# The end of a routed-expert diffusion step: the last expert's 128 rows gathered and normed apart from the other latents

## Chip, cores and metric

The kernel runs on one core of a Trainium2 chip. The metric is the device time of one execution in microseconds; three runs of the kernel before gave 2111.43 us as median (2108.97 to 2113.84).

## The reference, cut to what matters

One layer is computed for 128 prompt tokens and 1024 latent tokens of width 1024. The part that the change touches is the end of the mixture of experts and the final norm:

```python
gate, idx = lax.top_k(jnp.swapaxes(aff, 1, 2), cap)       # each of 16 experts picks its own 128 latents (16 prompt tokens)
xs  = h[idx]
hid = silu(xs @ w1[e]) * (xs @ w3[e])                     # 1024 -> 2048
out = (hid @ w2[e]) * gate[..., None]                     # 2048 -> 1024
y   = zeros.at[idx].add(out)                              # a token can be picked by several experts, or by none
x   = x + gate2 * y
y_prompt, y_sample = rmsnorm(x_prompt, final_g), rmsnorm(x_sample, final_g)
```

A latent that the last expert didn't pick has its final value once the fifteenth expert's rows are added. At most 128 of the 1024 latents change after that.

## The kernel before

`hybrid_step_kernel` first runs the token mixer and the routing (to about 800 us), and then a loop over the 16 experts (`for e in range(E)`), each with two products. The first makes the hidden units in four blocks `fb`, for `w1` and `w3`. The second makes the 1024 outputs in two halves `dh`, each in four steps `kq` over the 2048 hidden units; `n = 4 * dh + kq` counts them from 0 to 7. Weights come as 384 chunks of 1 MB over the SP queue into five `raw` buffers. ScalarE casts each to a high part (`split_hi`, L1291), VectorE takes the rest as a bf16 low part (`split_lo`, L1297), and the buffer that this frees gets the next load. `ahead(n)` does the splits that come before chunk `n`. TensorE multiplies high parts (`highs`, L1482) and low parts (`lows`, L1492) into PSUM; `sums` copies the low half out on ScalarE (`bs`, L1502) and adds it on VectorE (`ot`, L1503). Every engine executes its instructions in the order in which the program writes them (`tc.manual_schedule()`), so this order is set by hand.

`finish(e, ot)` turns an expert's outputs into rows: TensorE transposes, VectorE scales by the gate, and GpSimd's indirect DMA adds the 128 rows to `x3_d`, the latents in HBM (L1516). For the last expert (`e == E - 1`) the end is made differently:

- `last_hot` (GpSimd) builds one-hot matrices that place the 128 rows among the eight latent tiles of 128 rows.
- After step `n = 3`, `last_half` adds columns 0 to 511 to `x3_d` by an indirect DMA (L1568), and the eight loads of L1575 fetch the latents from there; they wait for that addition to land.
- `last_rows` and `last_add` place columns 512 to 767 (during the second half of the product) and 768 to 1023 (after it) by matmuls with the one-hot matrices (L1554) and add them to the tiles in SBUF (L1556).
- Then the eight latent tiles get their sums of squares (L1544, L1782, L1789), the norm's small steps (`go3`, L149 to L157), the multiplication by the norm and `final_g` (`last_out`: L1776 on VectorE, for tiles 4 and 8 L1773 on ScalarE and L1774 on GpSimd) and their stores (L1777).
- The prompt's second group of eight experts is added by `finish_prompt` (L1598 to L1607); the prompt's norm and store (L1815, L1816) are the last work.

Of the kernel before, what the change touches and what calls it, by code (L numbers as in the profile page):

```python
# [8 lines left out]
F32 = mybir.dt.float32  # L9
# [10 lines left out]
P = 128  # L20
# [29 lines left out]
def hybrid_step_kernel(ctx: ExitStack, tc: tile.TileContext, x_prompt, x_sample, state_lru, c, c_ctx,  # L50
# [114 lines left out]
    ss3 = const.tile([P, NT], F32, name="ss3")  # L165
    rs1, go1 = rms(ss1, "a", NT)
    rs2, go2 = rms(ss2, "b", NT)
    rs3, go3 = rms(ss3, "c", NT)
# [903 lines left out]
    tile1 = route.tile([P, 8], F32, name="tile1")  # L1072
    lgi2 = route.tile([P, 1], I32, name="lgi2")

    def constants():
# [8 lines left out]
        G.iota(tile1, pattern=[[P, 8]], base=-1, channel_multiplier=0, allow_small_or_imprecise_dtypes=True)  # L1084
# [76 lines left out]
    def list_make(pool, e, hot):  # L1161

        t = tp_tile()
        for i in range(8):
            PE.matmul(t[:, :5], hot[:, i, :], parts[:, i, e, :], start=i == 0, stop=i == 7)
        c = pool.tile([P, 8], F32, name="lc", bufs=1)
        V.tensor_copy(c[:, :5], t[:, :5])
        V.scalar_tensor_tensor(lgi[:, e:e + 1], c[:, 4:5], float(P), c[:, 3:4], op0=OP.mult, op1=OP.add)
        if e == E - 1:
            V.scalar_tensor_tensor(c[:, 5:6], c[:, 4:5], float(P), c[:, 3:4], op0=OP.mult, op1=OP.add)  # L1170
            V.tensor_scalar(lgi2, c[:, 5:6], 2.0, None, op0=OP.mult)
            V.tensor_scalar(tile1, tile1, c[:, 5:6], -1.0, op0=OP.subtract, op1=OP.mult)
        V.tensor_tensor(c[:, 6:7], c[:, 1:2], c[:, 2:3], op=OP.add)
        V.tensor_tensor(lgv[:, e:e + 1], c[:, 0:1], c[:, 6:7], op=OP.add)
# [345 lines left out]
    sq4 = ep.tile([P, 4, 3], F32, name="sq4")  # L1520
    last = {}

    def last_hot():
        last["oh"] = ew.tile([P, D], F32R, name="xg", tag="xg", bufs=1).rearrange("p (i t) -> p i t", i=8)
        for i in range(8):
            G.tensor_scalar(last["oh"][:, i, :], iof, tile1[:, i:i + 1], None, op0=OP.is_equal)
        jv = ep.tile([P, 2, 512], F32, name="jv", tag="x2")
        last["junk"], last["vals"] = jv[:, 0], jv[:, 1]

    def last_rows(ot, d0, d1):  # L1530

        n = (d1 - d0) * P
        cs = slice(d0 * P, d1 * P)
# [3 lines left out]
        v = last["vals"][:, :n]  # L1537
        V.scalar_tensor_tensor(v, t[:, :n], lgv[:, E - 1:], g2r[:, cs], op0=OP.mult, op1=OP.mult)
        last["hl"] = hl_ = ew.tile([P, 2, 512], F32R, name="rows", bufs=2)[:, :, :n]
        A.copy(hl_[:, 0], v)  # L1540
        V.tensor_tensor(hl_[:, 1], v, hl_[:, 0].bitcast(F32), op=OP.subtract)

    def last_square(i, d0, d1, c):
        A.activation(last["junk"][:, :(d1 - d0) * P], x3s[i // 2][:, i % 2, d0 * P:d1 * P], AF.Square,  # L1544
                     accum_out=sq4[:, i, c:c + 1])

    def last_add(t, i0, d0, d1, c):

        n = (d1 - d0) * P
        cs = slice(d0 * P, d1 * P)  # L1550
        m = 512 // n
        for i in range(m):
            for a in range(2):
                PE.matmul(t[:, i * n:(i + 1) * n], last["oh"][:, i0 + i, :], last["hl"][:, a], start=a == 0, stop=a == 1)  # L1554
        x = x3s[i0 // 2][:, i0 % 2:i0 % 2 + m, cs]
        V.tensor_tensor(x, x, t.rearrange("p (i d) -> p i d", i=m), op=OP.add)  # L1556
        if c == 1 and i0 < 4:
            for i in range(m):
                last_square(i0 + i, d0, d1, c)

    def last_half(ot):

        rows = ew.tile([P, D], F32, name="rows", bufs=2)[:, :512]
        t = tp_tile()
        for k in range(4):
            PE.transpose(t[:, k * P:(k + 1) * P], ot[:, k, :CAP], ident)
        V.scalar_tensor_tensor(rows, t, lgv[:, E - 1:], g2r[:, :512], op0=OP.mult, op1=OP.mult)
        G.indirect_dma_start(out=x3_d.rearrange("r (h d) -> (r h) d", h=2),  # L1568
                             out_offset=bass.IndirectOffsetOnAxis(ap=lgi2, axis=0),
                             in_=rows, in_offset=None, compute_op=OP.add)  # L1570
        for h in (1, 0):
            for p in range(4):
                if h:
                    x3s[p] = ew.tile([P, 8, 256], F32, name="raw", bufs=RB).rearrange("p a b -> p (a b)")                         .rearrange("p (i d) -> p i d", i=2)
                SY.dma_start(x3s[p][:, :, h * 512:(h + 1) * 512],  # L1575
                             x3_d[p * 2 * P:(p + 1) * 2 * P, h * 512:(h + 1) * 512].rearrange("(i p) d -> p i d", p=P))

    def last_sums(ot):
        for _ in range(4):
            yield  # L1580
        last_rows(ot, 4, 6)
        yield
        for i in (0, 4):
            last_add(tp_tile(), i, 4, 6, 1)
            last_add(tp_tile(), i + 2, 4, 6, 1)
            yield

    def finish_prompt(g):

        oh = ep.tile([P, P], F32R, name="oh")  # L1590
# [3 lines left out]
        for h in range(2):  # L1594
            pr.append(ew.tile([P, 2, 512], F32R, name="rows", bufs=2))
# [3 lines left out]
            A.activation(pr[h][:, 0], t, AF.Copy, scale=pgv[:, g:g + 1])  # L1599
            V.scalar_tensor_tensor(pr[h][:, 1], t, pgv[:, g:g + 1], pr[h][:, 0].bitcast(F32), op0=OP.mult, op1=OP.subtract)  # L1600
        yield
        for h in range(2):
            hs = slice(h * 512, (h + 1) * 512)
            t = tp_tile()
            for a in range(2):
                PE.matmul(t, oh, pr[h][:, a], start=a == 0, stop=a == 1)
            V.tensor_tensor(x2p[:, hs], x2p[:, hs], t, op=OP.add)  # L1607

# [23 lines left out]
    for e in range(E):  # L1632
# [73 lines left out]
        for dh in range(2):  # L1706
            for kq in range(4):
                n = 4 * dh + kq
                step = None if quarter is None else lambda r: next(quarter, None)
                if (e, dh) == (E - 1, 1):  # L1710
# [135 lines left out]
```

## Time and profile before

| | us |
|---|---|
| median of three runs | 2111.43 |
| the profiled execution, as timed | 2112.77 |
| its span in the trace | 2111.0 |
| PE busy in the span | 2043.4 |
| DVE busy in the span | 1710.9 |
| ACT busy in the span | 1366.0 |
| last matmul of the last expert's products ends | 2079.21 |

A line such as L1776 is a line of the kernel before; PE is TensorE, DVE VectorE, ACT ScalarE, POOL GpSimd, and SP the queue of the sync engine. Times in the trace count from the start of the span. PEclk is the share of full speed that TensorE was granted.

### The profile page before, as it was taken

How to read it: one execution, taken by the hardware profiler on the slowest of the kernel's cores; microseconds unless marked ns; L12 is line 12 of the kernel's file. 1: busy time of each engine (PE TensorE's matmuls, PEld its weight loads, DVE VectorE, ACT ScalarE, POOL GpSimd, SP SyncE). 2: the span in 40 equal slices, each digit the busy share in tenths (PEclk: the TensorE clock that was granted, in tenths of full speed). 3: DMA queues.
4: the chain of work that ended last, by engine and by line, in shares of the span. 5: the costliest groups of instructions: out<-in, count | busy, mean ns of one | idle time of the engine just before them, and what ended most of it. 6: DMA issues, size and time to landing. Idle time of an engine off the chain costs nothing.

```text
span 2111.0 us, 40842 instructions
## 1 busy us (share of the span) xinstructions
PE 2043.4 (97%) x17397; PEld 1968.8 (93%) x17397; DVE 1710.9 (81%) x1913; ACT 1366.0 (65%) x1442; POOL 203.6 (10%) x337
## 2 busy tenths in 40 slices
PE   7999999999999997999999999999999999999995
PEld 4899998999999876899999999999999999999994
DVE  7788988732236377999999999998999899999896
ACT  7477675322112236777877877877877887787783
POOL 0000001010102121010010010011011011001031
PEclk9999999999999998999999999999999999999997
DMA  8143434164655348999999999999999999999985
GB/s 271 57 120 117 125 116 121 52 203 144 189 168 178 118 145 306 317 323 323 345 337 325 344 329 330 348 349 326 335 345 325 345 348 329 343 342 332 344 310 184
DMA packets 304821, 543.93 MB, mean 258 GB/s; under 512 B 16299, under 2 KB 85627, under 8 KB 304638
## 3 DMA queue, kind: packets, MB, share of 16 engines
q1 hardware_dynamic: 285306, 478.56, 65.1%
q0 software_dynamic: 15728, 52.77, 8.6%
q10 hardware_dynamic: 3604, 9.98, 1.3%
q8 instruction: 136, 2.23, 0.4%
q14 instruction: 47, 0.39, 0.1%
HBM read 500.60 MB, written 40.67 MB: 256 GB/s over the span
## 4 chain that ended last, share of the span: by engine, by line
PE 88%; DVE 7%; DMA 2%; ACT 1%; issue 1%; SPq 0%; DVEq 0%; ACTq 0%; POOLq 0%
PE ac L1482 37%; PE ac L1492 17%; PE a L196 6%; PE a L197 6%; PE a L195 6%; PE a L778 5%; DVE lo L1297 2%; PE a L1002 2%; PE a L1004 2%; PE a L1003 2%; DMA xg<-hn_d,lgi 1%; PE tp L667 1%; PE tp L1420 1%; PE tp L1040 1%; PE tp L1513 1%
## 5 line engine op out<-in xcount | busy, mean ns | idle before, releaser
L1297 DVE TENSOR_TENSOR lo<-raw,hi 128x2048 bf16<-128x2048 f32 x384 | 872.0, 2284 | 0.0
L1291 ACT CAST hi<-raw 128x2048 fp32r<-128x2048 f32 x384 | 729.4, 1912 | 9.1 <-DMA raw<-in_exp_w_dram 7.1
L1482 PE MATMUL ac<-x,hi 128*128 128x288 f32 x4096 | 585.5, 298 | 0.0
L1482 PEld LDWEIGHTS ac<-x,hi 128*128 128x128 f32 x4096 | 549.0, 188 | 1.0 <-issue 0.9
L1492 PEld LDWEIGHTS <-lo 128*128 128x128 bf16 x6144 | 382.6, 98 | 16.2
L1482 PE MATMUL ac<-hh,hi 128*128 128x288 f32 x2048 | 297.7, 298 | 0.0
L1502 ACT COPY bs<-ac 128x288 f32<-128x288 f32 x320 | 127.6, 399 | 246.4 <-PE ac L1482 131.6
L1492 PE MATMUL ac<-xb,lo 128*128 128x144 bf16 x4096 | 282.5, 226 | 0.0
L1482 PEld LDWEIGHTS ac<-hh,hi 128*128 128x128 f32 x2048 | 275.5, 188 | 0.0
L197 PE MATMUL a<-hn_hi,lo 128*128 128x384 f32 x624 | 210.5, 337 | 1.9 <-DVE lo L186 1.9
L195 PE MATMUL a<-hn_hi,hi 128*128 128x384 f32 x624 | 210.4, 337 | 0.0
L196 PE MATMUL a<-hn_lo,hi 128*128 128x384 f32 x624 | 210.2, 337 | 0.0
L1492 PE MATMUL ac<-hb,lo 128*128 128x144 bf16 x2048 | 146.8, 226 | 0.0
L186 DVE TENSOR_TENSOR lo<-raw,hi 128x1024 fp32r<-128x1024 f32 (+1 forms) x77 | 88.3, 1164 | 64.4 <-ACT hi L185 64.4
L1503 DVE TENSOR_TENSOR h<-ac,bs 128x288 f32<-128x288 f32 x256 | 115.3, 450 | 20.1 <-ACT bs L1502 19.8
L197 PEld LDWEIGHTS a<-hn_hi,lo 128*128 128x128 f32 x624 | 117.7, 189 | 2.2 <-DVE lo L186 2.2
L195 PEld LDWEIGHTS a<-hn_hi,hi 128*128 128x128 f32 x624 | 118.0, 189 | 0.4
L196 PEld LDWEIGHTS a<-hn_lo,hi 128*128 128x128 f32 x624 | 118.0, 189 | 0.0
L185 ACT CAST hi<-raw 128x1024 fp32r<-128x1024 f32 (+1 forms) x77 | 75.9, 1002 | 46.8 <-PE a L196 36.6
L1759 POOL TENSOR_TENSOR yps<-ot,modc 128x128 f32<-128x128 f32 x16 | 36.0, 2248 | 720.0 <-DVE ot L1503 720.0
L1503 DVE TENSOR_TENSOR ot<-ac,bs 128x288 f32<-128x288 f32 x64 | 29.2, 457 | 56.5 <-ACT bs L1502 56.5
L701 ACT ACTIVATE sg<-a 128x1152 f32<-128x1152 f32 x16 | 18.2, 1135 | 78.9 <-PE a L197 78.8
(439 smaller groups left out, 2648.2 us busy)
## 6 DMA issues: line engine op xcount, KB each, us to landing
raw<-in_exp_w_dram SPq DMA_DIRECT2D x380, 1024.0 KB, 7.4
raw<-in_w_in_dram SPq DMA_DIRECT2D x28, 512.0 KB, 4.7
raw<-in_w_mod_dram SPq DMA_DIRECT2D x28, 512.0 KB, 5.8
araw<-in_w_mod_dram SPq DMA_DIRECT2D x18, 256.0 KB, 7.2
g_d<-sg ACTq DMA_DIRECT2D x8, 576.0 KB, 3.3
yh_d<-yh POOLq DMA_DIRECT2D x8, 576.0 KB, 3.1
yl_d<-yl POOLq DMA_DIRECT2D x8, 576.0 KB, 4.6
m_d<-sg POOLq DMA_DIRECT2D x8, 576.0 KB, 4.2
```

Source lines behind the costliest of these rows:

```text
L185: A.copy(h, raw)
L186: V.tensor_tensor(l, raw, h.bitcast(F32), op=OP.subtract)
L195: PE.matmul(out, whi, xhi, start=first, stop=False)
L196: PE.matmul(out, whi, xlo, start=False, stop=False)
L197: PE.matmul(out, wlo, xhi, start=False, stop=last)
L778: PE.matmul(a3[:, ch, :CH], w[:, k, :], y[:, k, cs], start=n == 0 and k == 0 and w is hi, stop=n == 1 and k == KD - 1 and w is ws[-1])
L1291: A.copy(hl[n][0], raw[n])
L1297: V.tensor_tensor(lo, r, hi.bitcast(F32), op=OP.subtract)
L1482: PE.matmul(a[:, r, :2 * S], w[0][:, k, c0 + r * P:c0 + (r + 1) * P], x2(kk), start=kk == first, stop=kk == last)
L1492: PE.matmul(a[:, r, S:2 * S], w[1][:, k, c0 + r * P:c0 + (r + 1) * P], xb(kk), start=False, stop=kk == last)
L1502: A.copy(b, a[:, :, S:2 * S])
L1503: V.tensor_tensor(dst, a[:, :, :S], b, op=OP.add)
```

## The change

The eight latent tiles, with the rows of the first fifteen experts, are loaded whole while the last expert's second product runs (`last_load`; the first load goes into the buffer of `x2`, the others into `raw` buffers). They are normed, multiplied by `final_g` in place and stored to `y_sample` (`last_squares`, `go3`, `last_out`), spread over the steps `n` by `last_step`. The last expert's 128 rows are gathered once from `x3_d` (`xe`); `last_cols` adds the expert's outputs to them in three column groups and takes their squares, and after the product they get a norm of their own and are scattered by an indirect DMA over the rows of `y_sample` that were already stored. The one-hot matrices, their matmuls and the two index tables that they needed are gone. `finish_prompt` multiplies with plain fp32 operands (two matmuls) in place of a high and a low part (four). At step `n = 3`, `last_cols`, `prompt_sums` and the first part of `finish_prompt` now stand ahead of the last `ahead`, and with it ahead of the last chunk's low part.

```diff
-    def last_half(ot):
...
-        G.indirect_dma_start(out=x3_d.rearrange("r (h d) -> (r h) d", h=2),
...
+    def last_loads():
+        last["fg"] = ep.tile([P, D], F32, name="fg", tag="xp")
+        A.dma_start(last["fg"], bass.AP(tensor=final_g.tensor, offset=final_g.offset, ap=[[0, P], [1, D]]))
+        last["junk"] = ew.tile([P, D], F32, name="rows", bufs=2)
+        last["vals"] = ep.tile([P, 512], F32, name="vals", tag="h0")
+        last_load(0)
+        last["xe"] = ep.tile([P, D], F32, name="xe", tag="xf")
+        G.indirect_dma_start(out=last["xe"], out_offset=None, in_=x3_d[:, :],
+                             in_offset=bass.IndirectOffsetOnAxis(ap=lgi[:, E - 1:E], axis=0))
+        last_load(1)
+        last_load(2)
+
+    def last_load(p):
+        if p:
+            x = ew.tile([P, 8, 256], F32, name="raw", bufs=RB).rearrange("p a b -> p (a b)").rearrange("p (i d) -> p i d", i=2)
+        else:
+            x = ep.tile([P, 2, D], F32, name="x30", tag="x2")
+        x3s[p] = x
+        SY.dma_start(x, x3_d[p * 2 * P:(p + 1) * 2 * P, :].rearrange("(i p) d -> p i d", p=P))
+
+    def last_squares(p):
+        for i in range(2):
+            A.activation(last["junk"], x3s[p][:, i], AF.Square, accum_out=ss3[:, 2 * p + i:2 * p + i + 1])
+
+    def last_out(p):
+        for i in range(2):
+            n, x = 2 * p + i, x3s[p][:, i]
+            V.scalar_tensor_tensor(x, x, rs3[:, n:n + 1], last["fg"], op0=OP.mult, op1=OP.mult)
+            SY.dma_start(y_sample[0, n * P:(n + 1) * P, :], x)
+
+    def last_cols(ot, d0, d1, c, early=None):
+        n, cs, xe = (d1 - d0) * P, slice(d0 * P, d1 * P), last["xe"]
+        t = tp_tile()
+        for k in range(d0, d1):
+            PE.transpose(t[:, (k - d0) * P:(k - d0 + 1) * P], ot[:, k, :CAP], ident)
+        if early is not None:
+            early()
+        V.scalar_tensor_tensor(last["vals"][:, :n], t[:, :n], lgv[:, E - 1:], g2r[:, cs], op0=OP.mult, op1=OP.mult)
+        V.tensor_tensor(xe[:, cs], xe[:, cs], last["vals"][:, :n], op=OP.add)
+        A.activation(last["junk"][:, :n], xe[:, cs], AF.Square, accum_out=sqe[:, c:c + 1])
+
+    def last_step(n):
+        if n == 0:
+            last_loads()
+        elif n == 1:
+            last_load(3)
+        elif n == 2:
+            last_squares(0)
+        elif n == 3:
+            last_squares(1)
+            go3(slice(0, 4))
+        elif n == 4:
+            last_out(0)
+            last_squares(2)
+        elif n == 5:
+            last_out(1)
+            last_squares(3)
+        elif n == 6:
+            last_cols(ot, 4, 6, 1)
+            go3(slice(4, 8))
+            last_out(2)
+            last_out(3)
...
-                ahead(base + kq + 1 + AH)
                 if (e, n) == (E - 1, 3):
-                    last_half(ot)
+                    last_cols(ot, 0, 4, 0)
+                    prompt_sums(0, G)
                     fp = finish_prompt(1)
                     next(fp)
-                    quarter = last_sums(ot)
...
+                ahead(base + kq + 1 + AH)
+                if e == E - 1:
+                    last_step(n)
...
+    fg, xe = last["fg"], last["xe"]
+    first = slice(0, 512)
     next(fp)
+    prompt_sums(1, V)
+    last_cols(ot, 6, 8, 2, lambda: (next(fp), V.tensor_tensor(xe[:, first], xe[:, first], fg[:, first], op=OP.mult)))
+    V.tensor_reduce(ss3[:, 9:10], sqe[:, 0:3], axis=AX.X, op=OP.add)
+    go3(slice(9, 10), (0,))
+    next(fp)
+    next(fp)
+    go3(slice(9, 10), (1,))
+    A.activation(xe[:, first], xe[:, first], AF.Copy, scale=rs3[:, 9:10])
+    V.scalar_tensor_tensor(xe[:, 512:], xe[:, 512:], rs3[:, 9:10], fg[:, 512:], op0=OP.mult, op1=OP.mult)
+    G.indirect_dma_start(out=y_sample[0], out_offset=bass.IndirectOffsetOnAxis(ap=lgi[:, E - 1:E], axis=0),
+                         in_=xe, in_offset=None)
+    next(fp)
+    next(fp)
+    V.tensor_tensor(x2p[:, first], x2p[:, first], fg[:, first], op=OP.mult)
+    V.tensor_tensor(ss3[:, 8:9], sqe[:, 3:4], sqe[:, 4:5], op=OP.add)
+    go3(slice(8, 9))
+    A.activation(x2p[:, first], x2p[:, first], AF.Copy, scale=rs3[:, 8:9])
+    V.scalar_tensor_tensor(x2p[:, 512:], x2p[:, 512:], rs3[:, 8:9], fg[:, 512:], op0=OP.mult, op1=OP.mult)
+    SY.dma_start(y_prompt[0], x2p)
```

How the order of the instructions moves is shown at three places. The line numbers of the changed kernel differ by a few: L1291 became L1284, L1297 L1290, L1502 L1495, L1503 L1496.

The first place is ScalarE at the start of the last expert's second product: the casts of the last three chunks (`hi`) and the PSUM copies (`bs`) of its first half. Before:

```order
L1703 ACTIVATE ready<-ready 1x1
L1291 CAST hi<-raw 128x2048 x3
L1502 COPY bs<-ac 128x288 x2
L1747 DMA raw<-in_final_g_dram 128x1024
L1502 COPY bs<-ac 128x288
L1540 CAST rows<-jv 128x256
```

Now:

```order
L1706 ACTIVATE ready<-ready 1x1
L1284 CAST hi<-raw 128x2048
L1519 DMA fg<-in_final_g_dram 128x1024
L1284 CAST hi<-raw 128x2048 x2
L1539 ACTIVATE rows,ss_110<-x_24389 128x1024 x2
L1495 COPY bs<-ac 128x288 x2
L1557 ACTIVATE rows,sqe<-xe 128x512
L1539 ACTIVATE rows,ss_110<-raw 128x1024 x2
L150 ACTIVATE rr_c<-rv_c 128x4
L1539 ACTIVATE rows,ss_110<-raw 128x1024 x2
L1495 COPY bs<-ac 128x288
```

Two squares of whole latent tiles stand ahead of the two copies of the first half, and five more squares ahead of the third copy.

The second place is VectorE where the first half's outputs (`ot`) are done and one chunk's low part (`lo`) is left. Before:

```order
L1297 TENSOR_TENSOR lo<-raw,hi 128x2048 x3
L1503 TENSOR_TENSOR ot<-ac,bs 128x288 x2
L1297 TENSOR_TENSOR lo<-raw,hi 128x2048
L1567 SCALAR_TENSOR_TENSOR rows<-tp,lgv,g2r 128x512
L1591 TENSOR_SCALAR oh<-iof,pgf 128x128
```

Now:

```order
L1290 TENSOR_TENSOR lo<-raw,hi 128x2048 x3
L1496 TENSOR_TENSOR ot<-ac,bs 128x288 x2
L1555 SCALAR_TENSOR_TENSOR vals<-tp,lgv,g2r 128x512
L1556 TENSOR_TENSOR xe<-xe,vals 128x512
L1590 TENSOR_SCALAR oh<-iof,pgf 128x128
L1290 TENSOR_TENSOR lo<-raw,hi 128x2048
```

The last low part moved behind the three operations on the expert's rows.

The third place is VectorE during the second half of the product, between the third and the last output sums; only the new order is shown, since nothing of it stood there before:

```order
L1496 TENSOR_TENSOR ot<-ac,bs 128x288
L1544 SCALAR_TENSOR_TENSOR raw<-raw,rr_c,fg 128x1024 x2
L1555 SCALAR_TENSOR_TENSOR vals<-tp,lgv,g2r 128x256
L1556 TENSOR_TENSOR xe<-xe,vals 128x256
L149 TENSOR_SCALAR rv_c<-ss_110 128x4
L153 RECIPROCAL rq_c<-rr_c 128x4
L154 TENSOR_TENSOR rq_c<-rq_c,rv_c 128x4
L155 TENSOR_TENSOR rq_c<-rq_c,rr_c 128x4
L156 TENSOR_SCALAR rq_c<-rq_c 128x4
L157 RECIPROCAL rr_c<-rq_c 128x4
L1544 SCALAR_TENSOR_TENSOR raw<-raw,rr_c,fg 128x1024 x4
L1496 TENSOR_TENSOR ot<-ac,bs 128x288
```

All eight multiplications of the latent tiles (two stand just ahead of the piece) come before the last `ot`, with which the work on the last quarter of the product begins.

## Rows read from the trace of the kernel before

**Rows 1.** Windows: us, busy of PE, PEld, DVE, ACT, POOL, granted clock, DMA share, GB/s

```profile
2050.00:2060.00 10.00, 10.00 (x108) 9.79 (x107) 10.00 (x6) 9.33 (x8) 0.00 (x0) 1.00 0.39 141
```

**Rows 2.** The chain that ended last, in order of time: start us, us, what

```profile
2072.46 7.96 DMA raw<-x_d
```

**Rows 3.** Timeline of PE, second half of the last product: start us, us, operation

```profile
2062.87 2.38 PE L1482 MATMUL ac<-hh,hi 128*128 128x288 f32 x16
2065.09 2.17 PE L1492 MATMUL ac<-hb,lo 128*128 128x144 bf16 x32
...
2077.99 1.22 PE L1482 MATMUL ac<-hh,hi 128*128 128x288 f32 x8
```

**Rows 4.** Timeline of ACT, end of the last product's first half

```profile
2053.84 5.51 ACT L1291 CAST hi<-raw 128x2048 fp32r<-128x2048 f32 x3
...
2061.73 0.40 ACT L1502 COPY bs<-ac 128x288 f32<-128x288 f32 x1 [1.21 <-PE ac L1482]
```

**Rows 5.** Timeline of DVE at the same place

```profile
2062.53 2.28 DVE L1297 TENSOR_TENSOR lo<-raw,hi 128x2048 bf16<-128x2048 f32 x1
2064.73 0.75 DVE L1567 SCALAR_TENSOR_TENSOR rows<-tp,lgv,g2r 128x512 f32<-128x512 f32 x1
...
2065.40 0.28 DVE L1591 TENSOR_SCALAR oh<-iof,pgf 128x128 fp32r<-128x128 f32 x1
```

**Rows 6.** Timeline of the latent tiles' multiplications and squares after the product

```profile
2089.25 1.28 DVE L1776 SCALAR_TENSOR_TENSOR hi<-raw,rr_c 128x1024 f32<-128x1024 f32 x1
2090.45 0.68 DVE L1556 TENSOR_TENSOR raw<-raw,ac 128x512 f32<-128x512 f32 x1
2090.47 1.04 ACT L1782 ACTIVATE hi<-raw 128x1024 f32<-128x1024 f32 x1
...
2091.64 1.06 ACT L1782 ACTIVATE hi<-raw 128x1024 f32<-128x1024 f32 x1
```

**Rows 7.** Timeline of the small steps, the last quarter's and the prompt's

```profile
2081.12 0.45 DVE L1503 TENSOR_TENSOR ot<-ac,bs 128x288 f32<-128x288 f32 x1
...
2082.10 0.48 DVE L1538 SCALAR_TENSOR_TENSOR jv<-tp,lgv,g2r 128x256 f32<-128x256 f32 x1 [0.53 <-PE tp L1536]
...
2083.68 0.63 ACT L1544 ACTIVATE jv<-raw 128x512 f32<-128x512 f32 x1
...
2096.52 0.15 DVE L149 TENSOR_SCALAR rv_c<-ss 128x4 f32<-128x4 f32 x1
...
2097.77 0.18 DVE L157 RECIPROCAL rr_c<-rq_c 128x4 f32<-128x4 f32 x1
...
2102.55 1.27 DVE L1607 TENSOR_TENSOR x2p<-x2p,tp 128x512 f32<-128x512 f32 x2
...
2106.54 1.41 DVE L1815 SCALAR_TENSOR_TENSOR hi<-x2p,rr_c,raw 128x512 f32<-128x512 f32 x2
2107.32 0.99 SPq L1816 DMA_DIRECT2D out_dram<-hi  x2
```

**Rows 8.** DMA issues after 1990 us: out<-in, queue, count, KB each, median us to landing

```profile
raw<-in_exp_w_dram SPq DMA_DIRECT2D x19, 1024.0 KB, 6.4
raw<-x_d SPq DMA_DIRECT2D x8, 512.0 KB, 7.5
out_dram<-hi SPq DMA_DIRECT2D x8, 512.0 KB, 3.2
...
out_dram<-hi SPq DMA_DIRECT2D x2, 256.0 KB, 2.0
```

**Rows 9.** Line 1516, all fifteen experts' indirect additions: us to landing

```profile
DMA to landing us min/median/max: 6.1/7.6/9.6
```

**Rows 10.** Timeline of SP: the last weight loads

```profile
2000.95 48.75 SPq L1285 DMA_DIRECT2D raw<-in_exp_w_dram  x16
```

**Rows 11.** Timeline of PE: plain fp32 at 20 us, high and low parts at 1492 us

```profile
20.54 3.60 PE L386 MATMUL tp<-araw,sil 128*4 128x512 f32 x8
...
1491.78 1.09 PE L1606 MATMUL tp<-rows,oh 128*128 128x512 f32 x4
```

More of the change, by code (lines that the diff above doesn't have):

```diff
@@ L164, in hybrid_step_kernel @@
     ss2 = const.tile([P, NT], F32, name="ss2")
-    ss3 = const.tile([P, NT], F32, name="ss3")
+    ss3 = const.tile([P, NT + 1], F32, name="ss3")
     rs1, go1 = rms(ss1, "a", NT)
     rs2, go2 = rms(ss2, "b", NT)
-    rs3, go3 = rms(ss3, "c", NT)
+    rs3, go3 = rms(ss3, "c", NT + 1)
     pa = ExitStack()
@@ L1517, in finish @@
                              in_=rows, in_offset=None, compute_op=OP.add)
-    sq4 = ep.tile([P, 4, 3], F32, name="sq4")
+    sqe = ep.tile([P, 16], F32, name="sqe")
     last = {}
[L1523 to L1533, printed above, removed]
+    def last_loads():
[26 more added lines that the diff above has]
+        n, cs, xe = (d1 - d0) * P, slice(d0 * P, d1 * P), last["xe"]
         t = tp_tile()
@@ L1536, in last_rows @@
             PE.transpose(t[:, (k - d0) * P:(k - d0 + 1) * P], ot[:, k, :CAP], ident)
[L1537 to L1559, printed above, removed]
@@ L1561, in last_half @@
-    def last_half(ot):
[L1563 to L1567, printed above, removed]
-        G.indirect_dma_start(out=x3_d.rearrange("r (h d) -> (r h) d", h=2),
[L1569 to L1576, printed above, removed]
@@ L1604, in finish_prompt @@
             t = tp_tile()
-            for a in range(2):
-                PE.matmul(t, oh, pr[h][:, a], start=a == 0, stop=a == 1)
+            PE.matmul(t, oh, pr[h], start=True, stop=True)
+            if g:
+                yield
             V.tensor_tensor(x2p[:, hs], x2p[:, hs], t, op=OP.add)
+            if g:
+                A.activation(last["junk"][:, :512], x2p[:, hs], AF.Square, accum_out=sqe[:, 3 + h:4 + h])
+                yield
     find = search(1, 5)
@@ L1779, in hybrid_step_kernel @@
-    junk = ew.tile([P, 8, 256], F32R, name="hi", bufs=HB).rearrange("p a b -> p (a b)")[:, :D].bitcast(F32)
-    def last_squares(x, i):
-        A.activation(junk, x, AF.Square, accum_out=ss3[:, i:i + 1])
-    for i in range(4):
-        last_square(i, 0, 4, 0)
-    for i in range(2):
-        last_square(i, 6, 8, 2)
-        x = x3s[1][:, i, 768:]
-        V.scalar_tensor_tensor(last["vals"][:, :256], x, 1.0, x, op0=OP.mult, op1=OP.mult, accum_out=sq4[:, 2 + i, 2:3])
-    V.tensor_reduce(ss3[:, 1:5], sq4, axis=AX.X, op=OP.add)
```

88 lines of the change are left out of this document (17 added, 71 removed).

## Prediction

> **What bounds the kernel now.** I read the page first: PE is busy for 2043 of 2111 us, so up to the end of the last product only what PE does or waits for counts. Then I read the end alone, by the chain that ended last, the timeline of each engine and the landing times. The last matmul of the products starts its group at 2077.99 us and ends at 2079.21 [rows 3]; the span ends at 2111.0. For these 31.8 us PE is no longer the bound: the chain goes through the loads of the latents (7.96 us of waiting [rows 2]), then through VectorE, which works off the last additions, nine multiplications, three norms and the prompt's rows, each in turn. So the question is what the change leaves behind the last product, and whether what it puts ahead of that delays the product itself. Room there is: between 2050 and 2060 us the DMA engines are 39% busy, and the last weights are through [rows 1, 10].
>
> **The product, step by step.** The loads of the latents go out behind the last weight load, at about 2049.7 us [rows 10]. A load lands 6.4 us (weights) to 7.5 us (latents) after its issue [rows 8], so the first is there at 2056 to 2057.5; the others wait for `raw` buffers, at most until the casts end. Cost: nothing, hidden behind the casts of the last three chunks, which end at 2053.84 + 5.51 = 2059.35 [rows 4]. Without that cover ScalarE would stand still (a rival, below).
>
> ScalarE then squares two tiles ahead of the PSUM copies. Squares follow each other at 1.17 us [rows 6]: 2059.35 + 2.34 = 2061.7, two copies of 0.40 end at 2062.5 in place of 2062.13 [rows 4]. PE, which waits for them, resumes 0.4 us later: 2063.3 in place of 2062.87 [rows 3].
>
> The last chunk's low part moves behind three VectorE operations: 0.75, then an addition that I price at 0.64 (half of the pair of 1.27 [rows 7]), 0.28, and then its own 2.28 [rows 5]. From 2063.3 that ends at 2067.2, in place of 2064.8. PE wants it after 16 high matmuls (2.22 us between two starts [rows 3]), 16 low ones (half of 2.17) and a few more: 2066.6. New stall: 0.6 us.
>
> In exchange the one-hot matmuls and PE's waits for loaded tiles leave the product. What is left of the second half is 4 x 2.22 + 2 x 2.17 = 13.2 us [rows 3], some 0.3 us of transposes and the stall: it ends at 2077.4, 1.8 us earlier than before.
>
> **VectorE beside it.** This is the term that decides. Low part done at 2067.2. ScalarE has by then squared the first group of the expert's rows (0.63 [rows 7]) from 2064.7 and two more tiles, until 2067.7. The norm's six small steps with ScalarE's root take from 2096.52 to 2097.95 in the rows, 1.43 us [rows 7]: 2069.1. Then the tiles' multiplications at 1.20 us each (2089.25 to 2090.45, with no GpSimd beside them [rows 6]): two end at 2071.5, the third `ot` (0.45 [rows 7]) at 2072.0, two more at 2074.4, the expert's columns 512 to 767 with two operations of 0.48 [rows 7] at 2075.4, square and norm again (0.6 + 1.43) at 2077.4, four more multiplications at 2082.2. Only then comes the last `ot`, done at 2082.65, though PE has had it ready since 2077.4. Before it ended at 2081.57. So the name of the change holds by half: the last two pairs of tiles are finished behind the product, and the last quarter leaves VectorE 1.1 us later than now.
>
> **The tail.** From 2082.65: a small operation of 0.15 and one of 0.7 ahead, the last columns with 2 x 0.48: 2084.5. ScalarE takes a prompt copy, then the square: 2085.4. A sum, the norm (1.43) and an addition of 0.64 between its steps: 2087.6. Half of the expert's rows on each of ScalarE and VectorE, 0.70 (half of 1.41 [rows 7]): 2088.3, where GpSimd issues the scatter. For the prompt: addition 0.64, a multiplication of 0.68 [rows 6], its square beside it, sum, norm, 0.70 more: the store is issued at 2092.05. It is 512 KB, which lands in 3.2 us [rows 8]. Before, the last store (256 KB, 2.0 us [rows 8]) was issued about 2108.0 [rows 7], so the span ends 1.0 us after landing. New end: 2092.05 + 3.2 + 1.0 = **2096.3**, or 14.7 us less than 2111.0.
>
> The scatter is shown by no row. The nearest, the experts' indirect additions of the same 512 KB, land 6.1 to 9.6 us after issue [rows 9]: 2094.4 to 2097.9, with 1.0 behind that 2095.4 to 2098.9. Below, a plain store's 3.2 us is the bound. I take under 7 us, since those additions run beside the weight stream and read their target too; then the prompt's store ends last. Bounds for the end: 2096.3 to 2098.9.
>
> **Edits with one answer.** The gather of 128 rows goes out when the fifteenth expert's rows have landed, long before its first use at 2064; its 0.5 MB passes beside weights that SP sends whenever a buffer is free. Its price lies between nothing and the 3.2 us of a store of this size; I take nothing, as the chunk's landing (6.4) is well inside the time from its issue to its cast. GpSimd's eight comparisons go, off the path. Three small VectorE operations of the lists go, under cover of PE.
>
> The prompt's first group is added inside expert 8, where PE is the bound: two plain fp32 matmuls in place of four. Eight plain ones of 512 columns took 3.60 us, 0.45 each; four of the others took 1.09, 0.27 each [rows 11]. So 0.9 in place of 1.09: no cost. The Trainium skill, "FP8 and Floating Point Precision", section "TensorE Precision Notes", says that true fp32 takes four passes through the array. By it, two would cost 8 x 0.27 = 2.2 us, 1.1 more than now, and the end would be 2097.4; the row, with four columns of weights where the new ones have 128, speaks for two passes.
>
> **The rivals.**
> 1. *The scatter ends last.* For it: its chain to landing is the longest of any store (9.6 us at worst [rows 9]), and 7.6 us, the middle of these rows, already ties. Against it: the weights are gone by then. Price: the end at 2098.9, a median of 2099.3.
> 2. *The latents are wholly hidden*, as the change says. Then the last `ot` follows PE's end by 0.40 + 0.45 and stands at 2078.25, 4.4 us earlier: a median of 2092.3. Against it: VectorE has 18.9 us of work (2063.3 to 2082.2) for 14.1 us of product, and its order puts the multiplications first.
> 3. *Slower: the first latent tile lands late.* The squares stand ahead of the PSUM copies on ScalarE, and a ScalarE that waits for the load holds the copies, the sums, PE's next transposes and the whole end, microsecond for microsecond from 2059.35. The kernel is no faster once that load lands 14.7 us past this, at 2074, and 0.2% slower at 2078.3: 28.6 us after issue, a median of 2115.7. For it: the load is right behind weights, and waits for the fifteenth expert's scatter and for `x2`. Against it: rows of 6.4 and 7.5 us [rows 8], and free DMA engines. Late by a few us is likelier: 3 us give a median of 2099.7.
> 4. *The change doesn't pay*, because work only changes places: VectorE would need 15 us more than the rows say. Against it: the loads' wait of 7.96 us [rows 2] and the one-hot splits, additions and two-engine multiplications are really gone.
>
> **The numbers.** The sum is against the profiled execution, timed at 2112.77 with a span of 2111.0; that stands 1.34 us above the median of the three runs. 2111.43 - 14.7 gives 2096.7. Chances: forecast 0.66, scatter last 0.18, wholly hidden 0.04, late load by a few us 0.06, no gain 0.03, slower 0.03. The forecast's own range is 2093 to 2099.5: 2 us either way for small steps that I rounded, and as much for runs, which lie 2.5 us from their median. Reaching to the scatter's and the late load's price gives 2092 to 2102. A measurement of this kernel can tell about 0.2%, 4.2 us; every case but the last two is faster by more: faster 0.94, same 0.03, slower 0.03.
>
> **What would show it.** In the profile after: PE's last product matmul ends near 2077.5, and PE then waits some 5 us for `ot`; VectorE works without a gap of a microsecond from 2063 to 2088; no wait of ScalarE for a latent load; the prompt's store issued near 2092 and the scatter landed before it. The prediction is wrong if ScalarE waits at its first square, if the last `ot` follows PE's end within a microsecond, or if the last event is the scatter's landing.

## The result, and the profile after

The changed kernel takes 2097.59 us (median of 4 runs, 2096.76 to 2098.41) against 2111.75 us for the kernel before on the same chip (4 runs): ratio 0.9933, 95% interval [0.9918, 0.9949]. The forecast was 2096.7 us, faster by more than 0.2%. The profiled execution spans 2095.2 us and was timed at 2096.98.

To compare executions I count from one **mark**: the last copy `bs` of the last expert's first product, behind which all that the change moves at the end lies. It stands at 2049.08 us before:

```profile
2049.08 0.40 ACT L1502 COPY bs<-ac 128x288 f32<-128x288 f32 x1 [0.69 <-PE ac L1482]
```

In the changed kernel the timeline of ACT has it at 2046.59 us. Columns as in [rows 4]: start, busy, operation, count, idle time before and what ended it.

```profile
2046.59 0.40 ACT L1495 COPY bs<-ac 128x288 f32<-128x288 f32 x1 [0.69 <-PE ac L1475]
...
2051.36 5.50 ACT L1284 CAST hi<-raw 128x2048 fp32r<-128x2048 f32 x3
2056.93 1.06 ACT L1539 ACTIVATE rows<-x 128x1024 f32<-128x1024 f32 x1
...
2059.17 0.68 ACT L1495 COPY bs<-ac 128x288 f32<-128x288 f32 x2
```

The first square follows the casts without a wait: the first latent tile, issued at 2047.38, was just there. The timeline of PE:

```profile
2060.17 0.80 PE L1552 MATMUL tp<-ident,ot 128*128 128x128 f32 x4 [1.02 <-DVE ot L1496]
...
2064.94 0.92 PE L1485 MATMUL ac<-hb,lo 128*128 128x144 bf16 x12 [0.57 <-DVE lo L1290]
...
2072.18 2.36 PE L1475 MATMUL ac<-hh,hi 128*128 128x288 f32 x16
...
2080.30 0.69 PE L1552 MATMUL tp<-ident,ot 128*128 128x128 f32 x2 [5.33 <-DVE ot L1496]
...
2081.63 3.63 PE L1606 MATMUL tp<-pr,oh 128*128 128x512 f32 x4
```

The stall on the last low part is 0.57 us, the products end at 2074.53, and PE then waits 5.33 us for the last `ot`. The timeline of DVE shows why:

```profile
2065.69 0.17 DVE L149 TENSOR_SCALAR rv_c<-ss 128x4 f32<-128x4 f32 x1 [0.81 <-ACT rows L1539]
...
2075.00 4.87 DVE L1544 SCALAR_TENSOR_TENSOR raw<-raw,rr_c,fg 128x1024 f32<-128x1024 f32 x4
2079.79 0.45 DVE L1496 TENSOR_TENSOR ot<-ac,bs 128x288 f32<-128x288 f32 x1
...
2083.67 0.69 DVE L1609 TENSOR_TENSOR x2p<-x2p,tp 128x512 f32<-128x512 f32 x1 [0.34 <-PE tp L1606]
...
2085.24 0.75 DVE L1777 SCALAR_TENSOR_TENSOR xe<-xe,rr_c,fg 128x512 f32<-128x512 f32 x1
...
2089.03 0.75 DVE L1786 SCALAR_TENSOR_TENSOR x2p<-x2p,rr_c,fg 128x512 f32<-128x512 f32 x1
```

Four of the latents' multiplications (1.22 us each) stand ahead of the last `ot`. Behind it comes the tail: the expert's rows are ready at 2085.99, the prompt's at 2089.78. The issues on POOL and SP, and the times to landing:

```profile
2086.81 1.27 POOL L1778 DMA_INDIRECT out_dram<-xe,lgi  x1 [25.96 <-DVE x2p L1609]
```

```profile
2089.84 0.33 SPq L1787 DMA_DIRECT2D out_dram<-x2p  x1
```

```profile
raw<-x_d SPq DMA_DIRECT2D x3, 1024.0 KB, 8.8
out_dram<-raw SPq DMA_DIRECT2D x6, 512.0 KB, 2.7
...
out_dram<-xe,lgi POOLq DMA_INDIRECT x1, 3.6
```

The scatter landed at 2090.4, ahead of the prompt's store. Yet something of POOL ends last: a record named DRAIN on its queue. The view of the kernel's last line (count, duration in ns min/median/max, first and last start):

```profile
L1813 POOLq DRAIN  x3: 46/97/7838, 2086.6 to 2094.9; - x3
L1813 SPq DRAIN  x3: 7/7/7, 2092.9 to 2094.7; - x3
```

SP is through with its waits at 2092.9, but the long drain on POOL's queue, begun at 2086.6 when POOL reaches the scatter, ends 7.84 us later, at 2094.4; only then does the closing barrier go on. Before, the same view has

```profile
L1842 POOLq DRAIN  x3: 46/97/6963, 2099.2 to 2110.7; - x3
L1842 SPq DRAIN  x3: 7/7/7, 2110.2 to 2110.5; - x3
```

where the drain, from 2099.2 to 2106.2, was over 4 us before SP was through.

**Where the 15.8 us between the spans come from.** From the mark to the end: 61.9 us before, 48.6 now, a gain of 13.3. Before the mark the changed kernel is 2.5 us ahead. By the start of each chunk's low part, chunk against chunk, that is two things: 3.26 us gained ahead of expert 8 (1.12 us before 784 us, 1.96 us from there to 802 us, in the routing stretch, and 0.2 behind it; more on this at r10), and 0.78 us lost again in expert 8, where the prompt's first group is now added with plain fp32 matmuls.

### The profile page after: what moved, and what is told of

It is laid out like the page before. It is cut to its first block, busy times and chain, and to the rows that moved or that the text cites. A ratio compares the mean times of both kernels' runs of the same rounds, so it can differ in the third digit from the quotient of the medians.

```text
span 2095.2 us, 40732 instructions
## 1 busy us (share of the span) xinstructions
PE 2036.8 (97%) x17365; PEld 1961.8 (94%) x17365; DVE 1702.2 (81%) x1907; ACT 1365.5 (65%) x1437; POOL 188.0 (9%) x327
## 4 chain that ended last, share of the span: by engine, by line
PE 88%; DVE 7%; ACT 2%; DMA 1%; issue 1%; SPq 0%; ACTq 0%; DVEq 0%; POOLq 0%
PE ac L1475 36%; PE ac L1485 17%; PE a L196 6%; PE a L197 6%; PE a L195 6%; PE a L778 5%; DVE lo L1290 2%; PE a L1002 2%; PE a L1004 2%; PE a L1003 2%; DMA xg<-hn_d,lgi 1%; PE tp L667 1%; PE tp L1413 1%; PE tp L1040 1%; PE tp L1506 1%
## 5 line engine op out<-in xcount | busy, mean ns | idle before, releaser
L1290 DVE TENSOR_TENSOR lo<-raw,hi 128x2048 bf16<-128x2048 f32 x384 | 872.0, 2284 | 0.0
L1284 ACT CAST hi<-raw 128x2048 fp32r<-128x2048 f32 x384 | 729.7, 1912 | 7.0 <-DMA raw<-in_exp_w_dram 4.1
L1495 ACT COPY bs<-ac 128x288 f32<-128x288 f32 x320 | 127.3, 398 | 237.5 <-PE ac L1475 125.7
L1496 DVE TENSOR_TENSOR h<-ac,bs 128x288 f32<-128x288 f32 x256 | 115.6, 451 | 22.5 <-ACT bs L1495 22.5
L1496 DVE TENSOR_TENSOR ot<-ac,bs 128x288 f32<-128x288 f32 x64 | 29.1, 457 | 52.8 <-ACT bs L1495 52.8
```

The lines of the kernel that those rows point to most:

```text
L1284: A.copy(hl[n][0], raw[n])
L1290: V.tensor_tensor(lo, r, hi.bitcast(F32), op=OP.subtract)
L1495: A.copy(b, a[:, :, S:2 * S])
L1496: V.tensor_tensor(dst, a[:, :, :S], b, op=OP.add)
```

## The experiments

A kernel's own profile gives the times after the mark, in us; ratios are against the kernel before on the same chip. r1 to r4, r5 to r8, and r9 with r10 each ran on one chip, so across these groups the ratios are compared and not the medians.

| kernel | last `ot` done | end | median us | ratio, interval |
|---|---|---|---|---|
| before | 32.49 | 61.91 | | |
| changed | 33.65 | 48.61 | 2097.59 | 0.9933 [0.9918, 0.9949] |
| r1, four scalings out | 28.87 | 44.01 | 2093.48 | 0.9917 [0.9900, 0.9933] |
| r2, no scatter | 33.57 | 47.05 | 2095.92 | 0.9926 [0.9909, 0.9942] |
| r3, low part first | 35.35 | 50.32 | 2099.24 | 0.9947 [0.9930, 0.9963] |
| r4, group 0 in parts | 33.62 | 48.60 | 2096.68 | 0.9933 [0.9917, 0.9950] |
| r5, ACT and POOL scale | 34.43 | 51.05 | 2100.86 | 0.9964 [0.9950, 0.9978] |
| r6, r3 and squares first | 32.60 | 47.57 | 2098.71 | 0.9948 [0.9932, 0.9965] |
| r7, r4 + r5 + r6 | 33.91 | 50.51 | 2099.69 | 0.9955 [0.9938, 0.9971] |
| r8, first load late | 42.71 | 57.68 | 2108.07 | 0.9988 [0.9979, 0.9998] |
| r9, end reordered | 30.01 | 45.29 | 2095.15 | 0.9920 [0.9907, 0.9934] |
| r10, changed again | 34.72 | 49.67 | 2097.81 | 0.9940 [0.9927, 0.9954] |

### r1: is it DVE's order?

```diff
         for i in range(2):
             n, x = 2 * p + i, x3s[p][:, i]
-            V.scalar_tensor_tensor(x, x, rs3[:, n:n + 1], last["fg"], op0=OP.mult, op1=OP.mult)
+            if p < 2:
+                V.scalar_tensor_tensor(x, x, rs3[:, n:n + 1], last["fg"], op0=OP.mult, op1=OP.mult)
```

> Leaves out the norm's multiplication of latent rows 512 to 1023 (four DVE passes of 1.22 us, 4.87 us in the changed kernel); those rows are stored as loaded. Theory A (after the products the order on DVE bounds the end: the last ot stands behind these passes, PE waits 5.33 us for it): last ot ends about 4.9 us earlier, 28.8 us after the last bs of the first product in place of 33.65; every later step moves with it; end about 4.5 us earlier (44.1 after that bs, not 48.6), time about 2093.0 us. Rival B (the stores' landing or TensorE bounds the end): last ot earlier, but the end moves by under 1 us. Of the clock: if TensorE is slowed at the end because it stood idle 5.33 us, the four matmul records of the prompt's rows (3.63 us in the changed kernel) fall to about 2 us and the end gains up to 1.5 us more.

`ot` moved by 4.78 us and the end by 4.60: theory A. The products ended where they did, 27.95 after the mark (27.94 in the changed kernel), so it was not TensorE. The expectation on the clock was half right. PE's prompt matmuls now follow a wait of 0.55 us, and the timeline of PE has

```profile
2072.88 2.36 PE L1475 MATMUL ac<-hh,hi 128*128 128x288 f32 x16
...
2076.22 0.44 PE L1553 MATMUL tp<-ident,ot 128*128 128x128 f32 x2 [0.55 <-DVE ot L1496]
...
2077.47 1.98 PE L1607 MATMUL tp<-pr,oh 128*128 128x512 f32 x4 [0.28 <-DVE vals L1556]
```

1.98 us in place of 3.63, and the prompt's store is issued 8.8 us behind `ot`, not 9.6. But the end gained nothing more by it: from `ot` to the end it is 15.1 us here and 15.0 in the changed kernel. The scatter was the one held now: its operand was ready at 2081.08, but POOL issued it at 2083.15: the last of its waits, which by their semaphores are for the latents' stores, came at 2082.3.

```profile
L1779 POOLq EVENT_SEMAPHORE  x5: 43/43/3657, 2076.2 to 2082.3; - x5
```

### r2: what ends last?

The edit takes out the `G.indirect_dma_start` into `y_sample`.

> Leaves out the last scatter, so the 128 rows of the last expert keep what the prompt stores of latents gave them. Theory A (POOL's own last drain, which begins at the scatter and lasted 7.8 us, ends the program 1.46 us after SP was through): the end comes about 1.4 us earlier, some 47.1 us after the last bs of the first product, time about 2096.1 us; POOL's last drain is short. Rival B (the prompt's store and its landing end last anyway, and the drain only looks long): no change within 0.3 us.

The end came at 47.05, as theory A had it. The view of the last line:

```profile
L1811 POOLq DRAIN  x3: 46/97/4920, 2062.4 to 2095.4; - x3
L1811 SPq DRAIN  x3: 7/7/7, 2094.8 to 2095.1; - x3
```

POOL's drain takes 4.92 us even so, but begins when POOL reaches its last instruction, now at 2062, and costs nothing there. So a drain follows POOL's last instruction, scatter or not, and what counts is when that is issued. With the scatter it took 7.6 to 7.8 us in every profile, against 3.3 to 3.6 us to landing.

### r3 and r6: the low part, and ACT's order

```diff
                 if (e, n) == (E - 1, 3):
+                    last_squares(1)
+                ahead(base + kq + 1 + AH)
+                if (e, n) == (E - 1, 3):
                     last_cols(ot, 0, 4, 0)
...
-                ahead(base + kq + 1 + AH)
```

This is r6. r3 moves `ahead` alone: `last_squares(1)` stays behind `last_cols`.

> Puts the last low part (lo of the last weight piece, 2.28 us on DVE) ahead of the first columns of the expert's rows. Theory A (DVE and ACT bound the end, PE's stall of 0.57 us on lo is covered): PE's stall goes, its products end about 0.6 us earlier, but vals, xe and the square of xe come 2.3 us later, ACT does the squares of latents 2 and 3 behind it, and rv of the first norm comes 1.5 to 2.3 us later than 19.1 us after the last bs of the first product; last ot and the end about 1.5 us later, time about 2099 us. Rival B (TensorE bounds the end): the end comes 0.6 us earlier, time about 2097.0 us.

> The last low part first, as in r3_low_first, and the squares of latent rows 2 and 3 ahead of the square of xe on ACT, where ACT stood idle 2.72 us. Theory A (r3 lost its 1.7 us because ACT's squares of rows 2 and 3 waited behind xe's, which waited for lo): the first norm now comes about 1.3 us earlier than in the changed kernel, TensorE's stall of 0.57 us goes too, last ot about 32.3 us after the last bs of the first product (33.65 changed, 35.35 in r3), end about 47.2, time about 2096.2 us. Rival B (lo's 2.28 us on DVE is itself the price, ACT's order does not matter): last ot and the end stay at those of r3, 35.35 and 50.3.

In r3 PE's stall on the low part was gone and the last `ot` 1.70 us later. That does not decide about rival B, for the products ended no earlier: PE now stood for the third `ot`, and they ended at 28.8 after the mark, 0.8 us later. The timeline of PE in r3:

```profile
2071.20 0.44 PE L1552 MATMUL tp<-ident,ot 128*128 128x128 f32 x2 [1.22 <-DVE ot L1496]
```

That TensorE doesn't bound the end is shown by r1. In r6 the last `ot` was 1.05 us earlier than in the changed kernel, 2.75 earlier than in r3, with ACT's order alone between the two; the forecast of 32.3 was 0.3 short. The timelines of ACT, r3 and then r6:

```profile
2058.74 0.68 ACT L1495 COPY bs<-ac 128x288 f32<-128x288 f32 x2
2063.71 0.63 ACT L1557 ACTIVATE rows<-xe 128x512 f32<-128x512 f32 x1 [4.29 <-issue]
...
2064.47 1.06 ACT L1539 ACTIVATE rows<-raw 128x1024 f32<-128x1024 f32 x1
```

```profile
2059.68 0.68 ACT L1495 COPY bs<-ac 128x288 f32<-128x288 f32 x2
2060.25 1.07 ACT L1539 ACTIVATE rows<-raw 128x1024 f32<-128x1024 f32 x1
```

In r3 the squares of loaded rows stood 4.29 us behind a square that waited for DVE's `xe`, done there at 2063.63 (the view names no releaser). r6's gain of 1.0 us is seen in its profile alone; the medians (2098.71 and 2097.59) can't tell it.

### r4: the 0.78 us in expert 8

The edit gives group 0 its two parts again: `pr` and `oh` as fp32r, the rest `pr - high` made on DVE, two matmuls for each half.

> The prompt's first group (in expert 8) goes back to high and low parts; its second group, at the end, stays with plain fp32 matmuls. Theory A (a plain fp32 128x512 matmul takes about 0.87 us here and the 0.77 us that the changed kernel loses between 1463 and 1523 us is that): the loss goes, the offset to the kernel before keeps its value through expert 8, and the time is about 0.8 us lower, 2096.8 us, within the scatter of the runs. Rival B (the loss comes from something else in expert 8, a wait on rows or on ACT): the offset still shrinks by 0.5 to 0.8 us there, and the time stays.

The offset to the kernel before is now -4.18 us on both sides of expert 8; in the changed kernel it goes from -3.27 to -2.49. The timelines of PE there, changed and r4:

```profile
1488.51 1.88 PE L1606 MATMUL tp<-rows,oh 128*128 128x512 f32 x4
```

```profile
1487.61 1.09 PE L1616 MATMUL tp<-rows,oh 128*128 128x512 f32 x4
```

Both read "x4", but the changed kernel issues two matmuls and r4 four: a plain fp32 matmul leaves two records. One of these two matmuls takes 0.94 us, one with fp32r 0.27; the 0.79 us between the rows are the loss.

### r5: hand a row of each pair to ACT and POOL

```diff
+    def last_out_b(p):
+        n, x = 2 * p + 1, x3s[p][:, 1]
+        A.activation(x, x, AF.Copy, scale=rs3[:, n:n + 1])
+        G.tensor_tensor(x, x, last["fg"], op=OP.mult)
+        SY.dma_start(y_sample[0, n * P:(n + 1) * P, :], x)
...
```

It is called for the last three pairs, for which `last_out` keeps the first row alone.

> Of latent rows 3, 5 and 7 (blocks of 128) ACT scales by the norm (1.06 us for 128x1024) and POOL multiplies by the gain (about 2.35 us for 128x1024), so DVE does five of the eight passes of 1.22 us in place of eight. Theory A (DVE's order bounds the last ot): the second norm comes 1.2 us earlier and two passes fewer stand ahead of the last ot: it is done about 30.0 us after the last bs of the first product, not 33.65; end at about 45.0, time about 2094.0 us; the four matmul records of the prompt's rows take between 2.0 and 3.6 us, as TensorE waits about 1.7 us, not 5.3. Rival B (POOL and DVE slow each other, or the scatter waits for the row that POOL does last): the passes on DVE take longer than 1.22 us, or the scatter is issued later than 3 us after x2p's sum, and the end gains under 2 us.

Rival B, and worse than it said: DVE did three passes fewer and the last `ot` came 0.78 us *later*, the end 2.4. The timelines of POOL and of DVE:

```profile
2073.30 2.64 POOL L1544 TENSOR_TENSOR raw<-raw,fg 128x1024 f32<-128x1024 f32 x1 [11.11 <-ACT raw L1543]
2078.49 5.64 POOL L1544 TENSOR_TENSOR raw<-raw,fg 128x1024 f32<-128x1024 f32 x2 [2.55 <-DMA out_dram<-raw]
```

```profile
2073.61 2.37 DVE L149 TENSOR_SCALAR rv_c<-ss 128x4 f32<-128x4 f32 x1
...
2077.27 4.66 DVE L1550 SCALAR_TENSOR_TENSOR raw<-raw,rr_c,fg 128x1024 f32<-128x1024 f32 x2
2081.85 0.45 DVE L1496 TENSOR_TENSOR ot<-ac,bs 128x288 f32<-128x288 f32 x1
2082.33 1.88 DVE L1594 TENSOR_TENSOR yps<-ot,modc 128x64 f32<-128x64 f32 x1
```

An operation on 128x4 numbers, 0.17 us elsewhere, lasts 2.37 and ends at 2075.98, when POOL's multiplication (2073.30 + 2.64 = 2075.94) does. One on 128x64 lasts 1.88 in place of 0.23 and ends at 2084.21, with POOL's third (2084.13). `ot`, which reads PSUM, keeps its 0.45 beside POOL. The two passes of 2077.27 take 4.66 us together in place of 2.44. So each POOL multiplication stopped DVE, it did not relieve it: ahead of `ot`, two stops of 2.2 us each stand against three passes of 1.22 us that DVE no longer does, 0.7 us more. The Trainium skill, "SBUF — State Buffer", section "SBUF: two separate sides", says that VectorE and GpSimd hold a shared port pair as an exclusive lock for a whole instruction, and the later one blocks; of VectorE's operations it names those in a two-port mode or with two SBUF inputs. These rows agree: both DVE operations end with POOL's, to 0.1 us (the 128x4 one has a single SBUF input; in which mode it ran no row shows).

It holds the other way round too. Where the last low part is moved ahead (r3, r6, r7, r9), POOL's small multiplication, 0.29 us in the changed kernel, takes 2.26 us beside it. The timelines of DVE and POOL in r3:

```profile
2059.96 2.28 DVE L1290 TENSOR_TENSOR lo<-raw,hi 128x2048 bf16<-128x2048 f32 x1
```

```profile
2060.13 2.26 POOL L1584 TENSOR_TENSOR yps<-ot,modc 128x64 f32<-128x64 f32 x1 [43.87 <-DVE ot L1496]
```

And the kernel before had it: two DVE passes took 4.22 us where POOL multiplied (L1774) from 2090.64 to 2092.99.

```profile
2091.05 4.22 DVE L1776 SCALAR_TENSOR_TENSOR hi<-raw,rr_c 128x1024 f32<-128x1024 f32 x2
```

### r7: together

> r4, r5 and r6 together; the same output as the changed kernel's. Theory A (the three act on different steps): last ot about 28.7 us after the last bs of the first product, end about 43.4, expert 8 loses nothing, time about 2091.8 us. Rival B (TensorE's own products bound it once DVE is relieved): last bs stays at about 27.4 and ot at 27.9 at the earliest, so the two give no more than 5.8 us together; more than that would say that the steps behind ot shortened too (TensorE at full clock in the prompt's matmuls, up to 1.5 us).

Neither theory: r5's part took back more than r6's gave. r4's part held (the offset to the kernel before is -3.05 us on both sides of expert 8), and one small addition on DVE, 0.42 us elsewhere, took 2.54 us beside POOL:

```profile
2070.61 2.54 DVE L1562 TENSOR_TENSOR xe<-xe,vals 128x256 f32<-128x256 f32 x1
```

### r8: the rival that would have made it slower

The edit moves `last_load(0)` from the first step behind `last_load(3)` in the second.

> The load of latent rows 0 and 1 is issued last of the four (about 2056 us in place of 2047.4). Theory A (the rival of the prediction in which a late latent tile costs 1 us per us: its square stands on ACT ahead of the bs copies that free TensorE's accumulators): it lands 6 to 9 us after its issue, the first square starts at 15.5 to 18.5 us after the last bs of the first product in place of 10.34, bs and TensorE wait behind it, and the end comes 4 to 8 us later, 53 to 57, time about 2102 to 2106 us. Rival B (DVE's passes later on take it up): first square late by 5 us or more, end later by under 2 us.

Theory A, beyond its range. The load was issued at 2056.71; ACT's timeline:

```profile
2066.32 1.06 ACT L1538 ACTIVATE rows<-x 128x1024 f32<-128x1024 f32 x1 [8.81 <-DMA x<-x_d]
```

The first square started 9.6 us after the issue; it came 8.75 us later than in the changed kernel and the end 9.07: 1.04 us for each. Of the 14 us, 2.5 are left: the place of one load takes the rest.

### r9: a better order on DVE

r4 and r6, no POOL, and (cut to the core):

```diff
-            go3(slice(4, 8))
+            go3(slice(4, 8), (0,))
+            V.tensor_tensor(last["xe"][:, :512], last["xe"][:, :512], last["fg"][:, :512], op=OP.mult)
+            go3(slice(4, 8), (1,))
             last_out(2)
-            last_out(3)
...
-    last_cols(ot, 6, 8, 2, lambda: (next(fp), V.tensor_tensor(xe[:, first], xe[:, first], fg[:, first], op=OP.mult)))
+    last_cols(ot, 6, 8, 2, lambda: (next(fp), last_out(3, (0,))))
+    last_out(3, (1,))
```

The prompt's matmul of each half follows its copy `pr` at once (into `acc_pair()`), and both sums follow the scatter's operand.

> r4 and r6, and on DVE alone another order at the end (POOL multiplies nothing): of the eight passes the last two go behind the last ot, into the time in which DVE waits for TensorE's transposes and for ACT's square; the first half of xe by the gain goes into the wait of the second norm; the prompt's first half is multiplied as soon as its rows are there, and its two sums on DVE stand behind the scatter's operand. Theory A (DVE's order sets the end; there is idle time behind ot that two passes fit in at a cost of some 0.5 and 0.2 us): last ot about 29.9 us after the last bs of the first product (33.65 in the changed kernel), scatter issued about 6.9 us behind it, near 36.7 (40.2), POOL's drain ends about 7.6 us after that, end about 45.2 (48.6), time about 2093.5 us. Rival B (the scatter then waits for the landing of the last latent rows, stored only 3.6 us behind ot): scatter issued later than 7.5 us behind ot, end above 46. Rival C (TensorE slowed by standing idle keeps its last steps long): transposes and matmuls behind ot as long as in the changed kernel.

Theory A in the profile: `ot` at 30.01 (29.9 expected), the end at 45.29 (45.2), 3.3 us less than the changed kernel. Of rival B a little: the scatter's operand was ready at 2084.49, POOL's last wait ended at 2085.1 and the scatter went out at 2085.86, 7.1 us behind `ot`. Rival C failed: PE's granted clock is 1.00 from 2075 to 2085 us.

```profile
L1789 POOLq EVENT_SEMAPHORE  x5: 43/43/5034, 2076.8 to 2085.0; - x5
```

The median of 2095.15 is 2.7 us below that of the changed kernel beside it (r10); the intervals of the ratios overlap by a little, but all five runs of r9 (2092.22 to 2096.01) lie below all five of r10 (2097.44 to 2100.94). So the whole time fell too, by how much is not sharp, and r4's 0.78 us is part of it.

### r10: the changed kernel once more

> The changed kernel itself. Up to the routing stretch (784 to 801 us) it came 3.26 us earlier than the kernel before in its first profile; other kernels that share that code with it came 1.28 to 4.17 us earlier. Theory A (that stretch varies from run to run): the offset is again another one, anywhere from 0 to 4.5 us, the end after the last bs of the first product repeats at 48.6 within 0.1, and 0.78 us is again lost in expert 8. Rival B (the change moved something there): the offset repeats at 3.3 within 0.3. The time in either case: 2096 to 2099 us.

The offset ahead of expert 8 was -1.97, so not the first profile's -3.26, and 0.78 us were lost in expert 8 again. Over all profiles that offset lies between -0.36 (r9) and -4.17 us (r4) with the same code there. Instruction against instruction on ACT it has two parts. At 784 us it is -1.12 in the first profile, 0.17 in this one and between -2.3 (r6) and 0.7 (r2) in all, so that part is of the run. From there to 802 us both profiles of the changed kernel gain the same, 1.96 and 1.95 us, seven others 1.4 to 2.0, and r5 and r9 nothing. PE's granted clock goes with it: 0.70 before, in r5 and in r9, 0.80 to 0.86 in the others. The windows of before, r5 and the changed kernel (columns as in [rows 1]):

```profile
784.00:801.00 17.00, 13.11 (x67) 6.54 (x67) 13.37 (x45) 7.59 (x13) 7.27 (x9) 0.70 0.82 285
```

```profile
784.00:801.00 17.00, 14.27 (x69) 6.90 (x68) 13.32 (x43) 8.33 (x16) 9.15 (x10) 0.70 0.75 262
```

```profile
784.00:801.00 17.00, 12.70 (x70) 6.22 (x71) 15.29 (x49) 8.90 (x16) 10.15 (x10) 0.82 0.82 280
```

So the same code takes either form here. With one profile of before it stays open whether the change makes the faster one likelier.

But the end did not repeat: 49.67, not 48.61. The timelines of ACT and PE:

```profile
2059.06 1.06 ACT L1539 ACTIVATE rows<-x 128x1024 f32<-128x1024 f32 x1 [0.90 <-DMA x<-x_d]
```

```profile
2062.29 1.05 PE L1552 MATMUL tp<-ident,ot 128*128 128x128 f32 x4 [1.84 <-DVE ot L1496]
2062.99 3.64 PE L1475 MATMUL ac<-hh,hi 128*128 128x288 f32 x16
```

The first latent load was issued at 2048.68; its square could start 10.4 us later, and ACT waited 0.90 us for it. PE stood 1.84 us, and its next 16 matmuls took 3.64 us in place of 2.38: the mild form of rival 3, in an ordinary run.

## Why the prediction was right, and where it was not

Times after the mark, predicted from 2049.08 and measured:

| step | predicted | changed |
|---|---|---|
| first square starts | 10.3 | 10.34 |
| stall on the low part | 0.6 | 0.57 |
| products end | 28.3 | 27.94 |
| last `ot` done | 33.57 | 33.65 |
| scatter's operand ready | 39.2 | 39.40 |
| scatter issued | 39.2 | 40.22 |
| prompt's store issued | 42.97 | 43.25 |
| end | 47.2 | 48.61 |

- **The term that decides**, DVE's order ahead of the last `ot`, was right to 0.1 us, and r1, r3 and r9 show that it is the cause: `ot` and the end move together, in r1 while the products end where they did. That it is 0.1 us is partly luck: the first norm was done 0.5 us late (20.5 after the mark, 20.0 predicted), and the expert's columns and the second norm made it up. Rival 2 (latents wholly hidden) fell with that.
- **The end: the step "so the span ends 1.0 us after landing" failed.** Without the scatter it holds (r2: 47.05, predicted 47.2). With it POOL's drain ends last, about 1.5 us later. Rival 1 was wrong in its mechanism, and its price of 2.6 us was too high: the scatter lands in 3.6 us, close to a plain store's 3.2 [rows 8] and not at the indirect additions' 6.1 to 9.6 [rows 9]; it is the engine, not the transfer, that ends last.
- **"2088.3, where GpSimd issues the scatter" put nothing between the operand and the issue.** The operand was ready at 39.40, 0.2 us late; 0.8 us more pass before POOL issues it, here and in all seven other profiles in which the operand was the last that POOL waited for (the indirect additions of L1516: 0.28 us). As POOL's drain follows the issue, this counts in full: with the issue at 39.2 the end would have been 47.6, an estimate from these rows. The clock did less. PE's prompt matmuls took 3.63 us after its 5.33 us of standing idle, at a granted clock of 0.50 (the lower level, 1.2 GHz), but the sum that waits for them stands between two steps of the norm, and DVE waited 0.34 us for it. With 1.98 us in r1 the operand was ready 4.92 us behind `ot`, here 5.75. The windows (columns as in [rows 1]):

```profile
2075.00:2080.00 5.00, 0.00 (x0) 0.00 (x0) 5.00 (x5) 0.69 (x1) 0.00 (x0) 0.82 0.59 242
2080.00:2085.00 5.00, 4.70 (x10) 2.24 (x10) 3.43 (x12) 1.83 (x6) 0.00 (x0) 0.50 0.46 186
```

- **"0.45 each ... So 0.9 in place of 1.09: no cost" failed.** [Rows 11] count records, and a plain fp32 matmul leaves two: the eight records are four matmuls, 0.90 us each. Two cost 1.88 against 1.09, and 0.78 us were lost. The page of the Trainium skill that I weighed against that row, "FP8 and Floating Point Precision", section "TensorE Precision Notes", has four passes; by it the loss was put at 1.1 us. The trace agrees roughly: 0.94 us is 3.5 times 0.27. The row that I set against it was misread.
- **Rival 3** is real: 1.04 us per us in r8, 0.90 us of it in r10. The step "A load lands 6.4 us (weights) to 7.5 us (latents) after its issue" was too short: 9.6 and 10.4 us where ACT waits for the first tile (r8, r10), at most 9.55 in the changed kernel, which leaves no cover between the landing and the last cast. The weights' loads are of 1 MB too, so the size alone is not the reason; no run shows which it is.
- **The sum**: 14.7 us predicted from the mark on, 13.3 measured, 0.78 lost in expert 8, and the rest of the 14.2 us between the medians lies ahead of expert 8 and in the scatter of the runs. So the median came 0.9 us from the forecast partly by luck: errors of 2.2 us met a gain ahead of expert 8 that the prediction did not have.

## What to carry to other kernels

Where work is moved beside a product, list the queue of each engine behind it: what counts is not when TensorE ends, but what stands in that queue ahead of the last result. Work that has slack belongs into the waits behind it (r9), and a second engine helps only if it doesn't stop the first (r5). Count an engine's last drain among the ends of a program, and keep its last instruction early.

## What was not expected of the hardware

- POOL's drain at the program's end took 7.6 to 7.8 us from the scatter's issue, which landed in 3.3 to 3.6 us; 4.9 us without the scatter.
- A scatter's operand was ready 0.8 us before POOL issued it, where nothing else held it; for the indirect additions of L1516 it is 0.28 us.
- Each POOL multiplication of two tiles in SBUF (2.4 us where it started first) stopped DVE's operations on SBUF until it ended (r5, r7), and a DVE low part of 2.28 us stopped POOL (r3, r6, r7, r9).
- Idle times of 0.67 to 0.78 us between PE's last steps left the granted clock at 1.00 (r9, 2075 to 2085 us); after 1.84 us in r10 the stretch of 2060 to 2065 us has 0.74.
